# VectorE's weight sums in the Strassen-like FFN, each issued one split later

## The chip, the cores and the metric

One core of a Trainium2 chip runs the whole program in one launch. The metric is the device time in microseconds (us), the median of three runs. Engines are named as in the profile: PE (TensorE), PEld (its weight loads), DVE (VectorE), ACT (ScalarE), POOL (GpSimd), SP (the queue that issues most loads).

## The reference

Two layers act on x (256 tokens x 2048, float32): a token mixer (gated linear attention in the first, sparse attention in the second), then a SwiGLU FFN with 5632 hidden columns.

```python
for i in range(DEPTH):
    h = rmsnorm(x, norm_mix[i])
    x = x + mixer_i(h)
    x = x + swiglu(rmsnorm(x, norm_ffn[i]), ffn_w1[i], ffn_w3[i], ffn_w2[i])
return rmsnorm(x, norm_final)

def swiglu(h, w1, w3, w2):
    return (jax.nn.silu(h @ w1) * (h @ w3)) @ w2
```

The change touches the FFN alone.

## The kernel before

**Splitting.** Every float32 weight tile (128 x 2048, 1 MB, loaded by one DMA) is split in two for PE: `wh` is ACT's rounding copy (line 136), `wl` is DVE's remainder `raw - wh` (line 137). A product of a tile is then three matmuls for each 128 rows of it: hi x wh, hi x wl, lo x wh. `wh` and `wl` have three buffers each, plain weight loads (`raw`) four.

**The FFN.** The 11 column blocks of w1 and w3 (512 columns each) go block by block. Block 0 is multiplied plainly. Then come seven *turns*, numbered 0 to 6 in each layer (14 in all). A turn calls `pair` for one block: it forms h @ w1 and h @ w3 together with seven half products by a Strassen-like scheme, which needs sums of weight quarters. The quarters of a turn are four pairs of tiles: `va` (w1 top), `vb` (w3 top), `vc` (w3 bottom), `vd` (w1 bottom), each with tiles 0 and 1. `va` and `vb` stay in buffers of their own (`v0`, `v1`, `v2`, `g3`; which is which alternates by turn), `vc` and `vd` pass through the `raw` buffers.

`pair` is a generator with eight slots. Its products, in order: A11 (with va), F5 (with va after va += vb), F3 (with vc), A12 (with vd), F6 (with va, reloaded with an accumulating DMA), F7 (with vb after vb += vc), a slot without a product, and N22. Between two slots runs one step of other work: in turns 0, 3 and 6 a step of `plain_steps` (another block multiplied plainly, output `half`), in turns 1, 2, 4 and 5 a step of `pieces` (the FFN's second product, output `down`). Each step loads and splits one tile. These eight work tiles of a turn are called work 0 to work 7 here.

**The sums.** DVE makes four full-tile sums in a turn, at line 406: a0 and a1 (va[0] += vb[0], va[1] += vb[1]), which F5 needs, and b0 and b1 (vb[0] += vc[0], vb[1] += vc[1]), which F7 needs. `product` calls `then(c)` right behind `split_w` of tile c, so each sum is traced behind the split of its own product's tile. F6 and N22 get their sums from POOL's accumulating DMAs (line 409).

**What sets the order.** The Tile framework's scheduler takes instructions in traced order as priority and puts each on its engine's queue, ahead of others that it takes to be not ready; the queue then runs strictly in order. The loads on SP's queue wait for the buffer that they overwrite. The `raw` buffers go round: in each turn the order of these loads is work 0, work 1, vc[0], vc[1], work 2, vd[0], vd[1], work 3 and so on. So vd[1] waits for the last reader of vc[0], and work 3 for the last reader of vc[1]; these readers are the split and the sum (b0, b1).

Of the kernel before, what the change touches and what calls it, by code (L numbers as in the profile page):

```python
# [55 lines left out]
def trunk(  # L56
# [7 lines left out]
    nc = tc.nc  # L64
# [47 lines left out]


    side = deque()

    def tick():

        while side:
            try:
                return next(side[0])  # L120
            except StopIteration:
                side.popleft()
# [9 lines left out]
    def split_w(raw, pool=wp):  # L132

        wh = pool.tile([P, 4, NB], F32R, tag="wh", bufs=3 if pool is wp else 1, name="wh")
        wl = pool.tile([P, 4, NB], F32R, tag="wl", bufs=3 if pool is wp else 1, name="wl")
        nc.scalar.copy(wh, raw)  # L136
        nc.vector.tensor_sub(wl, raw, wh.bitcast(F32))  # L137
        return wh, wl

    def gemm_tail(w, c0, parts, pool, done):  # L140

        acc = [acc_p.tile([P, NB], F32, tag="acc", name=f"acc{t}") for t in range(NT)]
        tiles = []
        for gi, (hi, lo, r0) in enumerate(parts):
            raw = wp.tile([P, 4, NB], F32, tag="raw", bufs=RAW, name="raw")
            nc.sync.dma_start(raw, w[r0:r0 + 512, c0:c0 + NB].rearrange("(k p) n -> p k n", p=P))
            wh, wl = split_w(raw, pool if gi == 0 else wp)
            for k in range(4):
                tiles.append((hi, lo, k, wh[:, k, :], wl[:, k, :]))
        for t in range(NT):  # L150
            ts_ = slice(t * P, (t + 1) * P)
            for i, (hi, lo, k, wh, wl) in enumerate(tiles):
                nc.tensor.matmul(acc[t], hi[:, k, ts_], wh, start=i == 0, stop=False)
                nc.tensor.matmul(acc[t], hi[:, k, ts_], wl, start=False, stop=False)
                nc.tensor.matmul(acc[t], lo[:, k, ts_], wh, start=False, stop=i == len(tiles) - 1)
                if t == 0 and i % 2:
                    tick()
            done(t, acc[t])
# [210 lines left out]
    def pair(nrm, wa, wb, c0, turn, done):  # L369

        def src(w, j, c):
            r = j * 1024 + c * 512
            return w[r:r + 512, c0:c0 + NB].rearrange("(k p) n -> p k n", p=P)

        def load(w, j, homes):
            o = []
            for c, (pool, tag, bufs) in enumerate(homes):
                raw = pool.tile([P, 4, NB], F32, tag=tag, bufs=bufs, name=tag)  # L380
                nc.sync.dma_start(raw, src(w, j, c))
                o.append(raw)
            return o

        def product(acc, raws, form, start, stop, then=None):
            for c in range(2):
                wh, wl = split_w(raws[c])
                if then is not None:
                    then(c)
                hi, lo = nrm.forms[form]  # L390
                for j in range(4):
                    k = 4 * c + j
                    for i, (l_, r_) in enumerate(((hi, wh), (hi, wl), (lo, wh))):
                        nc.tensor.matmul(acc, l_[:, k, :], r_[:, j, :], start=start and k == i == 0,  # L394
                                         stop=stop and k == 7 and i == 2, skip_group_check=not start)
                    if j % 2:
                        tick()

        def bank():
            return acc_p.tile([P, NB], F32, tag="acc", name="acc")  # L400

        def sums(tag):
            return nrm.pool.tile([P, NB], F32, tag=tag, bufs=1, name=tag)

        def plus(dst, other):
            return lambda c: nc.vector.tensor_add(dst[c], dst[c], other[c])  # L406

        def plus_dma(dst, w, j):
            return lambda c: nc.gpsimd.dma_start(dst[c], src(w, j, c), accum_op=ALU.add)

        fz = nrm.pool
        stream = [(wp, "raw", RAW)] * 2
        homes = [((fz, "v0", 1), (fz, "v1", 1)), ((fz, "v2", 1), (res, "g3", 1))]
        va = load(wa, 0, homes[turn])
        vb = load(wb, 0, homes[1 - turn])
        b1 = bank()
        product(b1, va, "A11", True, True, plus(va, vb))
        s1 = sums("s1")
        nc.scalar.copy(s1, b1)
        yield  # L420
        b2 = bank()
        product(b2, va, "F5", True, True, plus_dma(va, wb, 1))
        y = sums("y")
        nc.vector.tensor_sub(y, b2, s1)
        yield
        vc = load(wb, 1, stream)
        product(b2, vc, "F3", False, True, plus(vb, vc))
        yield
        vd = load(wa, 1, stream)
        product(b1, vd, "A12", False, True)  # L430
        done("11", b1)
        yield
        b3 = bank()
        product(b3, va, "F6", True, True, plus_dma(va, wa, 1))
        w = sums("w")
        nc.vector.tensor_sub(w, b3, s1)
        nc.vector.tensor_add(w, w, b2)
        done("12", w)
        yield
        product(b3, vb, "F7", False, True)  # L440
        nc.vector.tensor_add(y, y, b3)
        yield
        yield
        product(b3, va, "N22", False, True)
        nc.vector.tensor_sub(s1, s1, b3)
        done("21", s1)
        done("22", y)
        yield

    def plain(nrm, ws, c0, done):  # L450

        for q, w in zip("12", ws):
            acc = [acc_p.tile([P, NB], F32, tag="acc", name="acc") for _ in range(3)]
            for g in range(4):
                raw = wp.tile([P, 4, NB], F32, tag="raw", bufs=RAW, name="raw")
                nc.sync.dma_start(raw, w[g * NB:(g + 1) * NB, c0:c0 + NB].rearrange("(k p) n -> p k n", p=P))
                wh, wl = split_w(raw)
                for bank, form, start, stop in ((0, "A11", True, True), (1, "F7", True, True)) if g < 2 else \
                        ((0, "A12", False, True), (2, "N22", True, True)):
                    hi, lo = nrm.forms[form]  # L460
                    for j in range(4):
                        k = 4 * (g % 2) + j
                        for i, (l_, r_) in enumerate(((hi, wh), (hi, wl), (lo, wh))):
                            nc.tensor.matmul(acc[bank], l_[:, k, :], r_[:, j, :], start=start and k == i == 0,  # L464
                                             stop=stop and k == 7 and i == 2, skip_group_check=not start)
                        if j % 2:
                            tick()
                if g == 1:
                    s1 = nrm.pool.tile([P, NB], F32, tag="s1", bufs=1, name="s1")
                    nc.scalar.copy(s1, acc[0])  # L470
                    nc.vector.tensor_add(s1, s1, acc[1])
                    yield
            nc.vector.tensor_sub(s1, s1, acc[2])
            done("1" + q, acc[0])
            done("2" + q, s1)
# [690 lines left out]
```

## Time and profile before

| what | us |
|---|---|
| median of three runs | 2260.61 (2259.99 to 2260.88) |
| the profiled execution | 2262.72 |
| its span | 2260.9 |
| PE busy in it | 2226.0 (98%) |
| DVE busy | 1576.4 (70%) |
| ACT busy | 1169.4 (52%) |
| DVE's 56 sums at line 406, each | 2.28 |

The profiled execution's time is 1.8 us above its span, and 2.1 us above the median of the runs. A busy PE in this table means that its matmuls overlap without a gap; the idle time that can be won is what the view of waits shows. The 40-slice picture shows PE at 9 tenths or more in all slices but the last, the granted clock at full, and the DMA engines mostly at 7 to 9 tenths in the FFN's slices.

### The profile page before, as it was taken

Reading aid. Unit: us, or ns where it says so; the run is one execution under the profiler, and the core shown is the slowest. Engines: PE = TensorE matmul, PEld = TensorE weight load, DVE = VectorE, ACT = ScalarE, POOL = GpSimd, SP = SyncE. Lnnn points to the kernel's source line nnn. Section 1 sums busy time; section 2 is a strip of 40 time slices with the busy share of each in tenths; the row PEclk is TensorE's granted clock in tenths of the full one; section 3 lists DMA queues with packets and bytes.
Section 4 is the critical chain, followed back from the end, with each engine's and each line's share of the span. In section 5 each row is a group of like instructions: output and inputs, shape, how many; then the busy total and the mean of one; then the engine's idle time right before and its main releaser. Section 6 shows DMA issues by size and latency. Waiting matters only on the chain.

```text
span 2260.9 us, 25126 instructions
## 1 busy us (share of the span) xinstructions
PE 2226.0 (98%) x10247; PEld 1834.7 (81%) x10247; DVE 1576.4 (70%) x1282; ACT 1169.4 (52%) x1046; POOL 100.1 (4%) x147
## 2 busy tenths in 40 slices
PE   9999999999999999999999999999999999999998
PEld 8888888887787887788888888888888778778787
DVE  6546455778878888876555755556887886887874
ACT  5545455555555555555444544555554555555553
POOL 0000000000000000000100000000000000000000
PEclk9999999999999999999999999999999999999999
DMA  8555465597797797795554555457779779779763
GB/s 289 169 170 188 128 229 184 200 290 223 231 290 219 233 276 228 230 264 179 176 181 150 185 169 168 160 194 242 200 212 313 212 217 310 213 219 304 222 203 111
DMA packets 250547, 484.96 MB, mean 214 GB/s; under 512 B 8072, under 2 KB 20704, under 8 KB 250304
## 3 DMA queue, kind: packets, MB, share of 16 engines
q1 hardware_dynamic: 219856, 423.33, 54.3%
q0 software_dynamic: 29568, 58.72, 15.0%
q8 instruction: 80, 1.31, 0.2%
q10 hardware_dynamic: 1008, 1.31, 0.2%
q14 instruction: 35, 0.29, 0.0%
HBM read 481.20 MB, written 2.12 MB: 214 GB/s over the span
## 4 chain that ended last, share of the span: by engine, by line
PE 81%; DVE 11%; DMA 3%; ACT 2%; issue 2%; SPq 0%; POOL 0%; POOLq 0%; ACTq 0%
PE acc L394 15%; PE acc L202 12%; PE acc L204 12%; PE acc L203 12%; PE half L494 9%; DVE wl L137 4%; PE down L552 4%; PE down L553 4%; PE down L551 4%; DMA raw<-in_ffn_w 3%; PE acc L464 3%; DVE v L406 2%; ACT wh L136 2%; DVE g L406 1%; DVE x L558 1%
## 5 line engine op out<-in xcount | busy, mean ns | idle before, releaser
L136 ACT CAST wh<-raw 128x2048 fp32r<-128x2048 f32 x187 | 358.0, 1915 | 439.4 <-PE down L553 164.3
L137 DVE TENSOR_TENSOR wl<-raw,wh 128x2048 fp32r<-128x2048 f32 x187 | 426.8, 2289 | 204.1 <-ACT wh L136 203.9
L193 DVE TENSOR_TENSOR wl<-raw,wh 128x2048 fp32r<-128x2048 f32 (+3 forms) x161 | 349.9, 2176 | 302.2 <-ACT wh L192 302.1
L192 ACT CAST wh<-raw 128x2048 fp32r<-128x2048 f32 (+3 forms) x161 | 291.9, 1816 | 261.5 <-PE acc L204 211.0
L202 PE MATMUL acc<-wh,hh 128*128 128x512 f32 (+3 forms) x832 | 325.5, 391 | 0.0
L204 PE MATMUL acc<-wh,hl 128*128 128x512 f32 (+3 forms) x832 | 317.3, 381 | 0.0
L203 PE MATMUL acc<-wl,hh 128*128 128x512 f32 (+3 forms) x832 | 316.3, 380 | 0.6 <-DVE wl L193 0.6
L137 DVE TENSOR_TENSOR wl<-v,wh 128x2048 fp32r<-128x2048 f32 x102 | 232.8, 2287 | 24.5 <-ACT wh L136 24.4
L136 ACT CAST wh<-v 128x2048 fp32r<-128x2048 f32 x102 | 195.2, 1913 | 76.6 <-PE acc L394 43.4
L552 PE MATMUL down<-wl,g 128*128 128x512 f32 x512 | 201.3, 393 | 13.7 <-DVE wl L137 13.5
L553 PE MATMUL down<-wh,g 128*128 128x512 f32 x512 | 199.6, 390 | 0.0
L551 PE MATMUL down<-wh,g 128*128 128x512 f32 x512 | 198.3, 391 | 0.0
L203 PEld LDWEIGHTS acc<-wl,hh 128*128 128x128 f32 x832 | 156.7, 188 | 29.5 <-issue 1.7
L204 PEld LDWEIGHTS acc<-wh,hl 128*128 128x128 f32 x832 | 156.3, 188 | 29.5
L202 PEld LDWEIGHTS acc<-wh,hh 128*128 128x128 f32 x832 | 156.5, 188 | 28.6 <-issue 1.9
L394 PE MATMUL acc<-wh,fhF 128*128 128x512 f32 x448 | 174.6, 390 | 0.0
L394 PE MATMUL acc<-wl,fhF 128*128 128x512 f32 x448 | 174.3, 389 | 0.0
L394 PE MATMUL acc<-wh,flF 128*128 128x512 f32 x448 | 174.3, 389 | 0.0
L202 PE MATMUL acc<-wh,g 128*128 128x512 f32 x424 | 167.0, 394 | 0.0
L203 PE MATMUL acc<-wl,g 128*128 128x512 f32 x424 | 165.8, 391 | 0.0
L204 PE MATMUL acc<-wh,g 128*128 128x512 f32 x424 | 165.6, 391 | 0.0
L552 PEld LDWEIGHTS down<-wl,g 128*128 128x128 f32 x512 | 96.1, 188 | 39.2 <-DVE wl L137 20.2
(311 smaller groups left out, 3608.5 us busy)
## 6 DMA issues: line engine op xcount, KB each, us to landing
raw<-in_ffn_w SPq DMA_DIRECT2D x208, 1024.0 KB, 7.0
raw<-in_dsa_w_in SPq DMA_DIRECT2D x48, 1024.0 KB, 5.0
v<-in_ffn_w SPq DMA_DIRECT2D x42, 1024.0 KB, 8.4
raw<-in_gla_w_in SPq DMA_DIRECT2D x40, 1024.0 KB, 5.1
v<-in_ffn_w POOLq DMA_DIRECT2D x40, 1024.0 KB, 9.0
raw<-in_gla_w_out SPq DMA_DIRECT2D x16, 1024.0 KB, 5.0
g<-in_ffn_w POOLq DMA_DIRECT2D x16, 1024.0 KB, 13.0
raw<-in_dsa_w_out SPq DMA_DIRECT2D x16, 1024.0 KB, 4.9
```

Source lines behind the costliest of these rows:

```text
L136: nc.scalar.copy(wh, raw)
L137: nc.vector.tensor_sub(wl, raw, wh.bitcast(F32))
L192: a = nc.scalar.copy(wh[:, sl, :n], raw[:, sl, :n])
L193: v = nc.vector.tensor_sub(wl[:, sl, :n], raw[:, sl, :n], wh[:, sl, :n].bitcast(F32))
L202: nc.tensor.matmul(acc[t][:, :n], hi[:, k, ts_], wh[:, k, :n], start=start, stop=False)
L203: nc.tensor.matmul(acc[t][:, :n], hi[:, k, ts_], wl[:, k, :n], start=False, stop=False)
L204: nc.tensor.matmul(acc[t][:, :n], lo[:, k, ts_], wh[:, k, :n], start=False, stop=last)
L394: nc.tensor.matmul(acc, l_[:, k, :], r_[:, j, :], start=start and k == i == 0, stop=stop and k == 7 and i == 2, skip_group_check=not start)
L494: nc.tensor.matmul(acc[bank], l_[:, k, :], r_[:, j, :], start=start and k == i == 0, stop=stop and k == 7 and i == 2, skip_group_check=not ...
L551: nc.tensor.matmul(acc[t], hi[:, k, ts_], wh[:, k, :], start=start, stop=False)
L552: nc.tensor.matmul(acc[t], hi[:, k, ts_], wl[:, k, :], start=False, stop=False)
L553: nc.tensor.matmul(acc[t], lo[:, k, ts_], wh[:, k, :], start=False, stop=last)
```

## The change

The four DVE sums of a turn are no longer traced behind their own tile's split. `plus` puts them into a queue, and `split_w` takes one from it behind the next split, whatever step that split belongs to. So a0 follows the split of va[1], a1 that of work 0, b0 that of vc[1], and b1 that of work 2, in traced order. No instruction is added or removed.

```diff
     side = deque()
+    sums_due = deque()
...
         wl = pool.tile([P, 4, NB], F32R, tag="wl", bufs=3 if pool is wp else 1, name="wl")
         nc.scalar.copy(wh, raw)
         nc.vector.tensor_sub(wl, raw, wh.bitcast(F32))
+        if sums_due:
+            sums_due.popleft()()
         return wh, wl
...
         def plus(dst, other):
-            return lambda c: nc.vector.tensor_add(dst[c], dst[c], other[c])
+
+            return lambda c: sums_due.append(lambda: nc.vector.tensor_add(dst[c], dst[c], other[c]))
```

In the built programs the order of the loads on SP and of POOL's accumulating DMAs is the same before and after. Turn 0 of each layer keeps its order on every engine. The other twelve turns are of two kinds.

**Turns 2, 3, 5, 6 of each layer (eight turns).** The start of turn 2 on DVE, before; `v2_4323` and `g3_4325` are va, `v0_4327` and `v1_4329` vb, `raw_4384` is work 0:

```order
L445 TENSOR_TENSOR s1_3843<-s1_3843,acc_4086 128x512
L406 TENSOR_TENSOR v2_4323<-v2_4323,v0_4327 128x2048
L584 SCALAR_TENSOR_TENSOR u_4287<-u_4287,rstd_3036,y_3912 128x512
L558 TENSOR_TENSOR x03_87<-x03_87,down0_4222 128x512
L558 TENSOR_TENSOR x13_88<-x13_88,down1_4223 128x512
L137 TENSOR_TENSOR wl_4364<-g3_4325,wh_4363 128x2048
L219 TENSOR_TENSOR g0_4322<-tr_4343,g0_4322 128x512
L406 TENSOR_TENSOR g3_4325<-g3_4325,v1_4329 128x2048
L219 TENSOR_TENSOR g0_4322<-tr_4356,g0_4322 128x512
L137 TENSOR_TENSOR wl_4387<-raw_4384,wh_4386 128x2048
L137 TENSOR_TENSOR wl_4416<-v2_4323,wh_4415 128x2048
```

The same place after (work 0 is now `raw_4383`):

```order
L449 TENSOR_TENSOR s1_3842<-s1_3842,acc_4086 128x512
L138 TENSOR_TENSOR wl_4363<-g3_4325,wh_4362 128x2048
L588 SCALAR_TENSOR_TENSOR u_4287<-u_4287,rstd_3036,y_3912 128x512
L562 TENSOR_TENSOR x03_87<-x03_87,down0_4222 128x512
L562 TENSOR_TENSOR x13_88<-x13_88,down1_4223 128x512
L410 TENSOR_TENSOR v2_4323<-v2_4323,v0_4327 128x2048
L222 TENSOR_TENSOR g0_4322<-tr_4342,g0_4322 128x512
L138 TENSOR_TENSOR wl_4386<-raw_4383,wh_4385 128x2048
L222 TENSOR_TENSOR g0_4322<-tr_4355,g0_4322 128x512
L410 TENSOR_TENSOR g3_4325<-g3_4325,v1_4329 128x2048
L138 TENSOR_TENSOR wl_4416<-v2_4323,wh_4415 128x2048
```

Sum a0 has moved behind the split of va[1], and a1 with the second `g` conversion behind the split of work 0. Further on in the same turn, DVE before, with `raw_4451` work 1, `raw_4483` and `raw_4485` vc, `raw_4523` work 2:

```order
L406 TENSOR_TENSOR v0_4327<-v0_4327,raw_4483 128x2048
L406 TENSOR_TENSOR v1_4329<-v1_4329,raw_4485 128x2048
L137 TENSOR_TENSOR wl_4454<-raw_4451,wh_4453 128x2048
L424 TENSOR_TENSOR y_4449<-acc_4414,s1_4380 128x512
L137 TENSOR_TENSOR wl_4488<-raw_4483,wh_4487 128x2048
L137 TENSOR_TENSOR wl_4505<-raw_4485,wh_4504 128x2048
L558 TENSOR_TENSOR x00_81<-x00_81,down0_4382 128x512
L558 TENSOR_TENSOR x10_82<-x10_82,down1_4383 128x512
L137 TENSOR_TENSOR wl_4526<-raw_4523,wh_4525 128x2048
```

and after:

```order
L410 TENSOR_TENSOR v0_4327<-v0_4327,raw_4483 128x2048
L138 TENSOR_TENSOR wl_4454<-raw_4451,wh_4453 128x2048
L428 TENSOR_TENSOR y_4449<-acc_4414,s1_4379 128x512
L138 TENSOR_TENSOR wl_4488<-raw_4483,wh_4487 128x2048
L138 TENSOR_TENSOR wl_4504<-raw_4485,wh_4503 128x2048
L562 TENSOR_TENSOR x00_81<-x00_81,down0_4381 128x512
L562 TENSOR_TENSOR x10_82<-x10_82,down1_4382 128x512
L410 TENSOR_TENSOR v1_4329<-v1_4329,raw_4485 128x2048
L138 TENSOR_TENSOR wl_4525<-raw_4522,wh_4524 128x2048
```

Sum b0 stays, b1 moves behind three splits and the two x updates. PE and ACT keep their order in these turns.

**Turns 1 and 4 of each layer (four turns).** They follow a turn with `plain_steps`. a0 and a1 move in the same way (the split of work 0 now comes ahead of a1 and of four `g` conversions). DVE's middle of turn 1 before, with `raw_3914` work 1, `raw_3946` and `raw_3948` vc, `raw_3986` work 2:

```order
L406 TENSOR_TENSOR v2_3775<-v2_3775,raw_3946 128x2048
L137 TENSOR_TENSOR wl_3917<-raw_3914,wh_3916 128x2048
L137 TENSOR_TENSOR wl_3951<-raw_3946,wh_3950 128x2048
L424 TENSOR_TENSOR y_3912<-acc_3877,s1_3843 128x512
L137 TENSOR_TENSOR wl_3968<-raw_3948,wh_3967 128x2048
L558 TENSOR_TENSOR x00_81<-x00_81,down0_3845 128x512
L558 TENSOR_TENSOR x10_82<-x10_82,down1_3846 128x512
L406 TENSOR_TENSOR g3_3777<-g3_3777,raw_3948 128x2048
L137 TENSOR_TENSOR wl_3989<-raw_3986,wh_3988 128x2048
```

and after:

```order
L138 TENSOR_TENSOR wl_3917<-raw_3914,wh_3916 128x2048
L410 TENSOR_TENSOR v2_3775<-v2_3775,raw_3946 128x2048
L428 TENSOR_TENSOR y_3912<-acc_3877,s1_3842 128x512
L138 TENSOR_TENSOR wl_3951<-raw_3946,wh_3950 128x2048
L138 TENSOR_TENSOR wl_3967<-raw_3948,wh_3966 128x2048
L562 TENSOR_TENSOR x00_81<-x00_81,down0_3844 128x512
L562 TENSOR_TENSOR x10_82<-x10_82,down1_3845 128x512
L138 TENSOR_TENSOR wl_3988<-raw_3985,wh_3987 128x2048
L410 TENSOR_TENSOR g3_3777<-g3_3777,raw_3948 128x2048
```

Both b0 and b1 stand one split later. In these four turns ACT also takes two `g` conversions ahead of its copy of va[1], and PE takes the eight transposes that feed them a few matmuls later.

## The prediction

> **What bounds the kernel now.** First the page's span and PE's busy row, then who PE waits for.
>
> ```profile
> span 2260.9 us, 25126 instructions
> PE 2226.0 (98%) x10247; PEld 1834.7 (81%) x10247; DVE 1576.4 (70%) x1282; ACT 1169.4 (52%) x1046; POOL 100.1 (4%) x147
> ...
> PE down L552 <- DVE wl L137: 13.5, 12, 1.6
> PE half L494 <- DVE wl L137: 7.3, 6, 1.6
> ```
>
> PE is idle for 34.9 us of the span, and 20.8 us of that in 18 waits, all at the first matmul of a work step that needs `wl` from DVE. Nothing else in the FFN makes PE wait for longer than a pipeline step, so only these 18 waits can be won back by reordering DVE. Next, where they are (timeline of PE):
>
> ```profile
> 531.76 0.50 PE L552 MATMUL down<-wl,g 128*128 128x512 f32 x1 [1.35 <-DVE wl L137]
> 616.77 0.50 PE L552 MATMUL down<-wl,g 128*128 128x512 f32 x1 [1.58 <-DVE wl L137]
> ...
> 1801.35 0.50 PE L552 MATMUL down<-wl,g 128*128 128x512 f32 x1 [0.47 <-DVE wl L137]
> ...
> 2109.59 0.50 PE L494 MATMUL half<-wl,fhA 128*128 128x512 f32 x1 [1.59 <-DVE wl L137]
> ```
>
> Twelve are at work 0, one in each turn but a layer's first: eight of 1.58 to 1.59 us (turns 2, 3, 5, 6; first and last shown are at 616.77 and 2109.59) and four of 1.35 to 1.39 us (turns 1 and 4; 531.76). The other six (1801.35 is one) are at work 3 and hold the rest, 20.8 − 8 x 1.59 − 4 x 1.37 = 2.6 us. Now DVE through the start of turn 2, where I follow the change:
>
> ```profile
> 604.16 0.68 DVE L445 TENSOR_TENSOR s<-s,acc 128x512 f32<-128x512 f32 x1
> 604.76 2.28 DVE L406 TENSOR_TENSOR v<-v,v 128x2048 f32<-128x2048 f32 x1
> 606.96 0.74 DVE L584 SCALAR_TENSOR_TENSOR u<-u,rstd,y 128x512 f32<-128x512 f32 x1
> 607.62 1.27 DVE L558 TENSOR_TENSOR x<-x,down 128x512 f32<-128x512 f32 x2
> 608.82 2.28 DVE L137 TENSOR_TENSOR wl<-g,wh 128x2048 fp32r<-128x2048 f32 x1
> 611.02 0.68 DVE L219 TENSOR_TENSOR g<-tr,g 128x512 fp32r<-128x512 f32 x1
> 611.62 2.28 DVE L406 TENSOR_TENSOR g<-g,v 128x2048 f32<-128x2048 f32 x1
> 613.83 0.69 DVE L219 TENSOR_TENSOR g<-tr,g 128x512 fp32r<-128x512 f32 x1
> 614.43 2.28 DVE L137 TENSOR_TENSOR wl<-raw,wh 128x2048 fp32r<-128x2048 f32 x1
> 616.63 2.28 DVE L137 TENSOR_TENSOR wl<-v,wh 128x2048 fp32r<-128x2048 f32 x1
> 618.84 2.28 DVE L137 TENSOR_TENSOR wl<-g,wh 128x2048 fp32r<-128x2048 f32 x1
> 621.04 4.49 DVE L406 TENSOR_TENSOR v<-v,raw 128x2048 f32<-128x2048 f32 x2
> 625.44 2.28 DVE L137 TENSOR_TENSOR wl<-raw,wh 128x2048 fp32r<-128x2048 f32 x1
> 627.64 0.68 DVE L424 TENSOR_TENSOR y<-acc,s 128x512 f32<-128x512 f32 x1
> 628.25 4.48 DVE L137 TENSOR_TENSOR wl<-raw,wh 128x2048 fp32r<-128x2048 f32 x2
> 632.65 1.27 DVE L558 TENSOR_TENSOR x<-x,down 128x512 f32<-128x512 f32 x2
> 635.04 2.29 DVE L137 TENSOR_TENSOR wl<-raw,wh 128x2048 fp32r<-128x2048 f32 x1 [1.12 <-ACT wh L136]
> ```
>
> DVE runs 30 us here without a gap: four sums fall together with nine splits. A full tile takes 2.28 us and lets the next start after 2.20; the small ones take 0.60 to 0.66. The split of work 0 (614.43) ends at 616.71, and PE starts 0.06 us later: sums a0 and a1 stand ahead of it. PE issues a matmul every 0.227 us and had issued three others after 614.34, so it could have gone on at 615.03: 1.74 us lost. Three more rows of PE, the first matmul with `wl` of work 1, 2 and 3:
>
> ```profile
> 627.78 0.50 PE L552 MATMUL down<-wl,g 128*128 128x512 f32 x1
> ...
> 638.56 0.39 PE L552 MATMUL down<-wl,g 128*128 128x512 f32 x1
> ...
> 649.44 0.39 PE L552 MATMUL down<-wl,g 128*128 128x512 f32 x1
> ```
>
> Work 1's is 0.2 us behind DVE's end at 627.72 and its pace; with the uneven step behind each stall, a turn of this kind loses about 2.1 us in all.
>
> **The change, part by part.** No instruction is added; 48 of the 56 sums move, 2.28 us each, so DVE's busy time stays. What counts is which split DVE finishes when.
>
> *Turns 2, 3, 5, 6, work 0 and 1.* I lay turn 2 out again in the new order with the steps above, from 604.16: s1; split of va[1] 604.76; u 606.96; x 607.62; a0 608.82; first `g` 611.02; split of work 0 611.62 to 613.90; second `g` 613.82; a1 614.42; splits of va 616.62 and 618.82; b0 621.02; split of work 1 623.22 to 625.50. ACT must keep up, since it needs a0 and a1 before it copies the new va:
>
> ```profile
> 611.40 1.92 ACT L136 CAST wh<-v 128x2048 fp32r<-128x2048 f32 x1 [0.80 <-ACT g L218]
> 613.22 0.57 ACT L218 CAST g<-tr 128x512 fp32r<-128x512 f32 x1
> ...
> 644.05 1.91 ACT L136 CAST wh<-raw 128x2048 fp32r<-128x2048 f32 x1 [0.64 <-PE down L553]
> ```
>
> a0 ends at 611.10, before ACT's copy at 611.40; the cast at 613.22 ends at 613.79, before the second `g`; a1 ends at 616.70, and ACT's copy of va[1], 1.9 us, at 618.7, just before its split at 618.82. So work 0 is there 1.1 us before 615.03, and that stall is gone. PE then wants work 1 at 627.6 − 2.0 = 625.6: it is there at 625.50. I count the gain up to here as 2.0 us a turn.
>
> *Work 2.* y goes at 625.5, the splits of vc at 626.2 and 628.4, the x updates at 630.7 (PE's matmuls for them end then, 2 us earlier than at 632.65), b1 at 631.9, the split of work 2 from 634.1 to 636.4. PE wants it at 638.56 − 2.0 = 636.5. The late b1 stands right ahead of it and uses up the cover: 0.1 us is left, and any slip shows here as a stall.
>
> *The loads.* SP's queue, and two windows around a hole between two accumulating loads (the last columns are PE's clock, the DMA engines' busy share and GB/s):
>
> ```profile
> 627.75 3.17 SPq L381 DMA_DIRECT2D raw<-in_ffn_w  x2
> 632.75 15.92 SPq L544 DMA_DIRECT2D raw<-in_ffn_w  x5
> ...
> 628.00:630.00 2.00, 2.00 (x10) 1.62 (x10) 2.00 (x2) 1.26 (x1) 0.43 (x1) 1.00 0.42 86
> 630.00:632.00 2.00, 2.00 (x11) 1.65 (x10) 2.00 (x2) 0.00 (x0) 0.87 (x1) 1.00 1.00 385
> ```
>
> vd[0] and vd[1] are issued when the splits of work 1 and vc[0] free their buffers, work 3 (first of the five) behind the split of vc[1], at 632.75. After the change vd goes 2.1 to 2.2 us earlier, but work 3 has to wait for b1's end at 634.2: 1.4 us later, 3.4 later against PE. Work 3 must land 4.3 us (ACT 1.9, DVE 2.3, handing on 0.1) before PE's 649.44 − 2.0. ACT took it at 644.05, when it had just landed; needed is 643.1. In the DMA engines' order work 3 runs behind vd[1] on the same queue, and the engines are full from 630 on, so its landing follows the work ahead of it. The hole (0.42 of 2 us busy, 1.2 us free) is filled by the earlier vd, which brings the landing to about 642.9: no stall in this turn. Turns with less room lose some: in turn 9 (1801.35) PE already waits 0.47 there, so with 1.2 us from the hole it would lose 2.0 − 1.2 = 0.8 of its lead. Between 0 and 0.8 I take 0.3, since only this one of the eight shows a wait there before. If the landing stayed where it was, this turn would lose 0.9 and turn 9 all 2.0, some 1.3 in the mean; if it followed the issue, 1.4 more, about 2.5.
>
> Sum: 8 x (2.0 − 0.3) = 13.6 us.
>
> *Turns 1 and 4.* Work 0's split, now ahead of a1, comes 2.2 us earlier or more and wins the 1.35 us of 531.76, 1.5 with the uneven step behind it. But here the loads are already late (SP, ACT and PEld in turn 1):
>
> ```profile
> 541.95 2.57 SPq L381 DMA_DIRECT2D raw<-in_ffn_w  x2
> 550.73 13.93 SPq L544 DMA_DIRECT2D raw<-in_ffn_w  x5
> ...
> 554.14 1.92 ACT L136 CAST wh<-raw 128x2048 fp32r<-128x2048 f32 x1 [1.73 <-DMA raw<-in_ffn_w]
> 560.02 1.91 ACT L136 CAST wh<-raw 128x2048 fp32r<-128x2048 f32 x1 [3.97 <-DMA raw<-in_ffn_w]
> ...
> 564.32 0.19 PEld L552 LDWEIGHTS down<-wl,g 128*128 128x128 f32 x1 [0.45 <-DVE wl L137]
> ```
>
> Work 3 is issued at 550.73, behind b1; vd[1] lands just before 554.14, work 3 just before 560.02, and PE waits 0.45. Now b1 goes behind the split of work 2: issue at about 552.6. That is still ahead of vd[1]'s landing, so I take the landing as unmoved; PE then comes 1.5 us earlier and waits 1.5 us longer. Gain 0; bounds +1.5 (it lands early enough) and −1.9 (it lands as much later as it is issued), four times.
>
> Here the Trainium skill bears, page "DMA: Bandwidth & Descriptors", section "Queues, rings and completion order": each DMA engine takes turns packet by packet between the queues that have work. By that rule, too, work 3 would land as its predecessors and POOL's load let it, and the four turns would give 0; the 5.9 us between the two landings, with POOL's load beside, agree.
>
> *The rest.* POOL's accumulating loads wait for the F5 splits of va (616.63 before, 616.62 now): not moved. Turn 0, the mixers and the tail keep their order: 0. Behind work 3 every split waits for PE's buffers, so a lead holds to the turn's end.
>
> From the profiled execution 2262.7 − 13.6 = 2249.1; its 2.1 us over the median are taken off: **2247 us**, −0.6%.
>
> **Rivals.**
> 1. *The loads cap the gain.* The hole isn't filled in time and work 3 lands where it did: 8 x (2.0 − 1.3) = 5.6 us, 2255. For it: the 0.47 at 1801.35 and 0.45 at 564.32. Against it: vd is released 2 us earlier.
> 2. *Everything is won.* Work 3 lands early in all twelve turns: 8 x 2.0 + 4 x 1.5 and the 2.6 of the six waits there, 24.6 us, 2236. The Trainium skill gives a way to it (same page, "Anatomy of one DMA"): 2.0 us plus bytes over 436 GB/s, by estimate 4.4 us for 1 MB. The trace differs: 9.3 us from 550.73 to 560.02. Little speaks for it.
> 3. *Slower.* Work 3's landing follows its issue. Then turns 1 and 4 lose 4 x 1.9 = 7.6, and the eight others end at 8 x (2.0 − 2.5) = −4: 2272. It turns slower where the landing moves by over about 1 us in all twelve turns. Against it: at its new issue its predecessor is still on the way.
> 4. *Nothing.* DVE's chain simply stalls PE later, at work 1 and 2, where I left 0.1 us: 2260 to 2263. Against it: DVE makes one sum less ahead of work 0 and one less ahead of work 1, and has 1.12 us of idle time at 635.04 to absorb.
>
> **How the numbers follow.** My sum 0.62; rival 1 0.16; rival 2 0.08; rival 3 0.06; rival 4 0.08. About 0.2% (4.5 us) is what a measurement of this kernel can tell from no change. Faster: my sum, rival 2 and most of rival 1, 0.84; the same: rival 4 and the rest of rival 1, 0.10; slower 0.06. The sum's own range is 2243 to 2252 (0.2 to 0.6 us a turn either way); with rival 1 and part of 2, leaving out 3, 4 and the ends, 2240 to 2256.
>
> **What would show it.** In the profile after, DVE's L410 and busy times are unchanged; PE's waits for `wl` at work 0 are gone in all twelve turns; what is left sits at work 3, 1 to 2 us in turns 1 and 4 and under 1 in most others, behind ACT copies that wait for a DMA. Stalls at work 1 or 2 would show rival 4; at work 3 over 2 us, rival 3. The prediction fails if DMA landings move by more than 1 us against my account, in either direction.

## The result, and the profile after

The changed kernel takes 2242.96 us in the median of four runs (2241.94 to 2246.99), the kernel before 2260.46 (2259.99 to 2260.88) beside it: a ratio of 0.9926 (95% interval 0.9909 to 0.9943), 17.5 us less. The forecast was 2247. The profiled execution after is the slowest of its four, 2246.99 us against 2262.72: 15.7 us less between the two traces, which are what the turns below are read from.

The page of the kernel after, its span and PE's row:

```profile
span 2245.2 us, 25136 instructions
...
PE 2222.0 (99%) x10247; PEld 1834.7 (82%) x10247; DVE 1573.2 (70%) x1282; ACT 1170.6 (52%) x1046; POOL 100.1 (4%) x147
```

PE's waits after (total us, number, longest):

```profile
PE down L556 <- DVE wl L138: 7.1, 7, 1.6
...
PE half L498 <- DVE wl L138: 1.6, 5, 0.6
```

20.8 us in 18 waits have become 8.7 us in 12. DVE's busy time is the same to about 3 us: it does the same work in another order. Where the twelve are, PE's timeline tells; of turn 2 it also shows the first matmul with `wl` of work 0, 1, 2 and 3:

```profile
563.61 0.50 PE L556 MATMUL down<-wl,g 128*128 128x512 f32 x1 [0.78 <-DVE wl L138]
...
613.87 0.39 PE L556 MATMUL down<-wl,g 128*128 128x512 f32 x1
...
624.98 0.40 PE L556 MATMUL down<-wl,g 128*128 128x512 f32 x1
...
635.88 0.39 PE L556 MATMUL down<-wl,g 128*128 128x512 f32 x1
...
647.64 0.50 PE L556 MATMUL down<-wl,g 128*128 128x512 f32 x1 [0.95 <-DVE wl L138]
...
1790.67 0.50 PE L556 MATMUL down<-wl,g 128*128 128x512 f32 x1 [1.59 <-DVE wl L138]
```

All twelve waits at work 0 are gone, none stands at work 1 or 2, and all that are left are at work 3 (563.61 is turn 1's, 647.64 turn 2's, 1790.67 the longest). Against the rows of before (616.77, 627.78, 638.56, 649.44) turn 2 is ahead by 2.90, 2.80, 2.68 and 1.80 us; 0.69 of that it brings along from the turns ahead, so it wins 2.2 at work 0, still holds 2.0 at work 2, and gives 0.9 back at work 3. Of the 2.2 some 0.45 is order and not time: before, three matmuls without `wl` stood ahead of this one (the two rows below), now one does (at 613.64). So PE's order does change a little in these turns, unlike what the section on the change says.

```profile
614.34 0.61 PE L551 MATMUL down<-wh,g 128*128 128x512 f32 x2
614.80 0.39 PE L394 MATMUL acc<-wh,fhF 128*128 128x512 f32 x1
```

DVE there, after:

```profile
608.13 2.28 DVE L410 TENSOR_TENSOR v<-v,v 128x2048 f32<-128x2048 f32 x1
610.33 0.68 DVE L222 TENSOR_TENSOR g<-tr,g 128x512 fp32r<-128x512 f32 x1
610.93 2.28 DVE L138 TENSOR_TENSOR wl<-raw,wh 128x2048 fp32r<-128x2048 f32 x1
613.13 0.69 DVE L222 TENSOR_TENSOR g<-tr,g 128x512 fp32r<-128x512 f32 x1
613.73 2.28 DVE L410 TENSOR_TENSOR g<-g,v 128x2048 f32<-128x2048 f32 x1
...
622.54 2.28 DVE L138 TENSOR_TENSOR wl<-raw,wh 128x2048 fp32r<-128x2048 f32 x1
```

The split of work 0 (610.93) runs ahead of a1 (613.73). With the 0.69 us added, each row lies within 0.1 us of the layout in the prediction (611.62, 614.42, 623.22).

Taken from the end of one turn to the end of the next (DVE's `s<-s,acc` row, 604.16 before and 603.47 after for turn 2's start), the turns became shorter by:

| turn | layer 1 | layer 2 |
|---|---|---|
| 1 | 0.84 | 0.81 |
| 2 | 0.98 | 1.07 |
| 3 | 1.85 | 1.76 |
| 4 | 1.36 | 1.12 |
| 5 | 2.08 | 0.86 |
| 6 | 1.68 | 1.34 |

The eight turns 2, 3, 5, 6 hold 11.6 us of it, the four turns 1 and 4 hold 4.1; turn 0 and all else come to 0.0 together.

### The profile page after: what moved, and what is told of

It is laid out like the page before. It is cut to its first block, busy times and chain, and to the rows that moved or that the text cites. A ratio compares the mean times of both kernels' runs of the same rounds, so it can differ in the third digit from the quotient of the medians.

```text
span 2245.2 us, 25136 instructions
## 1 busy us (share of the span) xinstructions
PE 2222.0 (99%) x10247; PEld 1834.7 (82%) x10247; DVE 1573.2 (70%) x1282; ACT 1170.6 (52%) x1046; POOL 100.1 (4%) x147
## 3 DMA queue, kind: packets, MB, share of 16 engines
q1 hardware_dynamic: 219856, 423.33, 54.9%
q0 software_dynamic: 29568, 58.72, 15.2%
HBM read 481.20 MB, written 2.12 MB: 215 GB/s over the span
## 4 chain that ended last, share of the span: by engine, by line
PE 83%; DMA 6%; DVE 6%; ACT 3%; issue 1%; SPq 0%; POOL 0%; ACTq 0%; POOLq 0%; DVEq 0%
PE acc L397 17%; PE acc L205 12%; PE acc L207 12%; PE acc L206 12%; PE half L498 10%; DMA raw<-in_ffn_w 6%; PE down L556 4%; PE down L557 4%; PE down L555 4%; DVE wl L138 4%; PE acc L468 3%; ACT wh L137 2%; PE tr L219 1%; DVE v L410 1%; PE trq L901 0%
```

## The experiments

All are edits of the changed kernel unless said otherwise, each timed beside the kernel before (medians of 2260.0 to 2261.7 us), given as a ratio to it. Two theories were on the table. Mine: PE's waits at work 0 went because one sum less stands ahead of that split, and what is left is set by work 3's landing, on DMA engines filled by an accumulating load. The rivals: the later b sums bring part of the gain, or work 3 waits for the plain loads ahead of it in its own queue.

### Which sums matter

With a0 and a1 alone put later:

```diff
+            def add(c):
+                nc.vector.tensor_add(dst[c], dst[c], other[c])
-            return lambda c: sums_due.append(lambda: nc.vector.tensor_add(dst[c], dst[c], other[c]))
+            return (lambda c: sums_due.append(lambda: add(c))) if dst is va else add
```

> Only a0 and a1 are put one split later; b0 and b1 are issued in the code where they were before. In the scheduled order DVE's sequence then equals the changed kernel's everywhere except in turns 1 and 4, where b1 goes ahead of the split of work 2 instead of behind it. Theory (the gain is work 0's split no longer standing behind a1; the b sums bring nothing of their own): 2243 us, within 2 us of the changed kernel; in turns 1 and 4 a wait of about 0.9 us at work 2 takes the place of the same amount at work 3. Rival (the later b sums bring part of the gain): 2248 to 2256 us. Rival by the prediction's account of turns 1 and 4 (b1's place sets work 3's issue, and its landing the turn): with b1 early again, work 3's issue is as before and turns 1 and 4 win 0.5 to 1 us more, 2239 to 2241 us.

Measured: 2245.34 us (2241.11 to 2245.87), ratio 0.9928 (0.9915 to 0.9940). The whole gain is there. The reverse, b0 and b1 alone, was not run, since in the built program the order of every engine is then the one of the kernel before. It is the scheduler that moves b1 behind three splits, as soon as the a sums stand later; the line in the code does not decide it. So in the eight turns DVE's order in this run is the changed kernel's, and the run does not say what b1's place there is worth. An estimate from turn 2 of the changed kernel: the split of work 1 ends at 624.82 and PE uses it from 624.98; with b1's 2.2 us still ahead of it, PE would wait about 2 us there. In the four turns where b1 does differ, PE loses 0.3 us at work 2 and less at work 3 than after the change, and the turns end alike. Work 3 is issued at 550.54 in turn 1, as in the changed kernel (550.58): b1's place does not set it, and the rival that let these turns win more is out.

With a1 alone (`dst is va and c == 1` as the condition):

> Only a1 is put one split later; a0 stands where it was before the change, ahead of the split of va[1]. In the scheduled order work 0's split is then again ahead of a1, and DVE's order from there on is that of the run with both a sums moved. Theory (work 0's split had 1.74 us of lateness and one sum of 2.2 us taken from ahead of it is enough): 2243 us, within 2 us of the changed kernel, no wait at work 0. Rival (both a sums must move, since va[1]'s first split comes 2.2 us later with a0 ahead of it and PE then waits there): 2250 us or more.

Measured: 2245.11 us (2241.39 to 2247.33), ratio 0.9929 (0.9916 to 0.9941). PE's waits in this run:

```profile
PE down L564 <- DVE wl L138: 2.8, 7, 0.7
PE half L506 <- DVE wl L138: 2.7, 3, 1.1
```

None is at work 0. One sum of 2.2 us out of the way is enough for a split that came 1.74 us late; in the code the other three need not move. The theory held, and it is narrower than the change. But in this run's trace, too, DVE has b1 behind the same three splits in the eight turns, so b1 did move.

### Turns 1 and 4 alone

The sums go later only where `turn in (1, 4)`:

> The sums are put one split later in turns 1 and 4 of each layer alone; the other turns keep the order of the kernel before. Theory (from the two traces turn by turn: turns 1, 4 of both layers end 0.84, 1.36, 0.81 and 1.12 us shorter): 4.1 us faster than before, about 2256.4 us, with the four waits at work 0 gone and the eight of 1.58 us left. Rival (the prediction's step: what is won at work 0 is lost again at work 3, net 0): 2260.5 us.

Measured: 2257.61 us (2256.10 to 2260.43), ratio 0.9989 (0.9980 to 0.9998), 0.5 to 4.5 us faster. By its trace the four turns are 0.86, 1.13, 0.70 and 0.35 us shorter than before, 3.0 in all. So the prediction's 0 for them was wrong, by somewhat less than the 4.1 us that the trace of the full change shows.

### What work 3 waits for

Without the second of the two accumulating loads behind F5, so that an addend of F6 and N22 is left out:

```diff
-        product(b2, va, "F5", True, True, plus_dma(va, wb, 1))
+        product(b2, va, "F5", True, True, lambda c: plus_dma(va, wb, 1)(c) if c == 0 else None)
```

> The changed kernel without the second accumulating load behind F5 (F6 and N22 then read va[1] without that addend): 14 MB less through the DMA engines, 8.7 us or more of them in each turn. Theory: the upper bound of what any placing of this load can bring: no wait at work 3, none at F6, 2231 to 2234 us. Rival (work 3 waits for the plain loads ahead of it): 2241 us or more.

Measured: 2234.67 us (2234.27 to 2234.89), ratio 0.9883 (0.9868 to 0.9898), and no wait for `wl` left in the FFN. The queues and issue groups, first of the changed kernel, then of this run (packets, MB and share of the 16 engines; KB each and median us from issue to landing):

```profile
q1 hardware_dynamic: 219856, 423.33, 54.9%
q0 software_dynamic: 29568, 58.72, 15.2%
...
raw<-in_ffn_w SPq DMA_DIRECT2D x208, 1024.0 KB, 7.8
```

```profile
q0 software_dynamic: 22176, 44.04, 11.7%
...
raw<-in_ffn_w SPq DMA_DIRECT2D x208, 1024.0 KB, 5.7
```

Of the changed kernel's 2245.2 us, 15.2% went into 56 accumulating loads, 6.1 us of all 16 engines each; 54.9% into 423 MB of plain loads, 3.1 us for each tile of 1.05 MB. An accumulating tile takes twice the engines' time of a plain one, and with 14 of them gone the FFN's plain loads land in 5.7 us in the median instead of 7.8. The 8.3 us that this run is faster I take as the most that any placing of this load can bring. The runs also agree within 0.6 us, those of the changed kernel within 5, so the spread from run to run seems to go with this load; how it arises, no run shows.

### Placing that load later

A first hold writes a small mark (a copy of 8 elements a partition) on POOL, ahead of the load. It reads `wl` of vd[0], and so waits for DVE's split of it:

```diff
+                    mark = sm.tile([P, 8], F32, tag="mark", bufs=1, name="mark")
+                    m = nc.gpsimd.tensor_copy(mark, last[0][:, 0, 0:8].bitcast(F32))
+                    with behind((m.ins,)):
+                        f(1)
```

> The changed kernel, with one wait more on POOL: the second of the two accumulating loads behind F5 (into va[1]) is held until DVE has split vd[0], some 9 us later. No instruction of the other engines moves. Theory (the accumulating load beside vd and work 3 takes the DMA engines' time and sets work 3's landing): work 3 lands 2 us earlier or more in every turn, the twelve waits there (about 10 us of lost issue time) go, the load lands near 649 us in turn 2, well ahead of F6's split of va[1]; 2232 to 2235 us. Rival A (work 3's landing follows from the plain loads ahead of it in its own queue, and the accumulating load beside matters little): 2241 to 2244 us. Rival B (the held load comes too late for F6 and makes a new wait there of 2 us or more in each turn): 2250 us or slower.

Measured: 2318.58 us (2317.08 to 2318.86), ratio 1.0255 (1.0241 to 1.0269). SP and POOL in turn 2, PE at F6, and four windows there (busy time of PE, PEld, DVE, ACT and POOL, PE's clock, DMA share, GB/s):

```profile
649.41 7.14 SPq L562 DMA_DIRECT2D raw<-in_ffn_w  x4
...
653.88 2.32 POOL L423 COPY mark<-wl 128x8 f32<-128x8 f32 x1 [17.84 <-DVE wl L138]
656.15 1.29 POOL L414 DMA_DIRECT2D g<-in_ffn_w  x1
...
673.13 0.49 PE L398 MATMUL acc<-wh,fhF 128*128 128x512 f32 x1 [1.97 <-ACT wh L137]
675.46 0.50 PE L398 MATMUL acc<-wl,fhF 128*128 128x512 f32 x1 [1.83 <-DVE wl L138]
...
672.00:674.00 2.00, 0.49 (x1) 0.19 (x1) 0.89 (x1) 2.00 (x2) 0.70 (x1) 1.00 0.31 24
674.00:676.00 2.00, 0.55 (x2) 0.50 (x3) 2.00 (x3) 2.00 (x2) 0.00 (x0) 0.97 1.00 169
676.00:678.00 2.00, 2.00 (x6) 1.52 (x6) 2.00 (x2) 0.69 (x1) 0.00 (x0) 0.50 1.12 206
678.00:680.00 2.00, 2.00 (x8) 1.58 (x7) 2.00 (x2) 0.14 (x1) 0.00 (x0) 0.68 0.80 137
```

The load left at 656.15, landed at 671.10, and PE stood still at F6 for 1.97 and 1.83 us, with one matmul between, which cost 4.2 us of issue time. Then it came back at a granted clock of 0.50: six matmuls in 2 us. Before the change, waits of 1.6 us caused no such drop. But a single wait of 1.83 us did in another run (the short hold everywhere, below), where one of 1.82 us did not (PE's rows, and a window behind each, with the same columns as above):

```profile
1704.23 0.76 PE L567 MATMUL down<-wl,g 128*128 128x512 f32 x1 [1.83 <-DVE wl L138]
...
1790.81 0.50 PE L567 MATMUL down<-wl,g 128*128 128x512 f32 x1 [1.82 <-DVE wl L138]
...
1706.00:1708.00 2.00, 2.00 (x7) 1.52 (x6) 2.00 (x2) 0.02 (x1) 1.22 (x1) 0.57 0.97 370
1792.00:1794.00 2.00, 2.00 (x11) 1.62 (x10) 2.00 (x2) 0.61 (x1) 0.64 (x1) 1.00 0.81 294
```

The Trainium skill, page "TensorE: Matmul & The Clock Gate", part 1, has a window of about 3.4 us without work after which PE falls to half its clock. The traces agree on the half, not on the length: neither of the two pauses in turn 2 nor the single one lasted 2.0 us, and why 1.83 us did it and 1.82 us did not is open.

Rival B held, though some 27 of the 76 us that this run is slower than the changed kernel come from the new tile (below). The theory's own part held too: work 3, issued at 649.41, landed at 654.26, in 4.9 us instead of 10.0, and no wait was left there.

The same hold in the kernel before:

> The same hold of the second accumulating load, in the kernel before, without the later sums. Theory: work 0's twelve waits stay, only the six waits at work 3 go (2.6 us, 3.2 us as lost issue time): about 2257 to 2258 us. So the hold is worth about 3 us here and some 9 us on the changed kernel: the later sums moved the bound to the loads. Rival (the loads cost PE the same in both kernels): 8 us or more faster here too, 2252 us or less.

Measured: 2303.66 us (2302.45 to 2305.38), ratio 1.0191 (1.0177 to 1.0205). Both expectations missed. The run tells nothing of what was asked, since late loads at F6 and the tile's shift (below) cover it.

Two shorter holds, to the split of vc[1] and to b1's end:

> The changed kernel; the second accumulating load behind F5 is held until DVE has split vc[1], 1.1 to 1.5 us later than it starts now, instead of 9 us and more as in the run held to vd[0]'s split. Theory (work 3's landing is set by how much of the second accumulating load runs ahead of it): work 3 lands about 1 us earlier, most of the waits there shrink by that, nothing is late at F6 (the load lands near 643 us in turn 2, needed by about 653): 2236 to 2240 us. Rival (any hold is paid back at F6): 2250 us or more. Rival (so short a hold does nothing): 2242 to 2245 us.

> As before it, but held until DVE has made sum b1, which in turns 2, 3, 5 and 6 is when work 3's own load is issued: 5 us later than now there, 7 us later in turns 1 and 4. Theory: work 3 lands about 3 us earlier, all waits there go; the load takes up to 15 us and lands near 648 us in turn 2 (needed by about 653) and near 567 us in turn 1 (needed by about 568): 2232 to 2236 us. Rival (the held load is late at F6 in turns 1 and 4, as in the run held to vd[0]): four waits of 1 to 3 us with a lower clock behind them, 2240 us or more.

Measured: 2271.36 us (2270.43 to 2272.54), ratio 1.0046 (1.0033 to 1.0059), and 2284.02 us (2281.82 to 2286.55), ratio 1.0102 (1.0088 to 1.0116). Both expectations missed, the first one strangely: its waits and PE's busy time are

```profile
PE down L567 <- DVE wl L138: 2.0, 4, 1.1
...
PE 2255.6 (99%) x10247; PEld 1838.5 (81%) x10247; DVE 1577.7 (69%) x1282; ACT 1171.3 (52%) x1046; POOL 110.2 (5%) x161
```

PE waits 6.7 us less than after the change, and yet the kernel is 28 us slower: PE is busy for 33.6 us more with the same 10247 matmuls, and over 6 us of that were lost ahead of the first FFN turn, where no hold is (block 0's last `s<-s,acc` on DVE starts at 446.73, after the change at 440.25). The new tile was left as the suspect. Of the second run it explains most, but not the waits at F6 in turns 1 and 4, of up to 1.8 us, which the rival had named.

### A tile of 32 bytes

The changed kernel with an unused tile, no instruction added:

```diff
+            if turn == 0:
+                sm.tile([P, 8], F32, tag="mark", bufs=1, name="mark")
```

> The changed kernel with the small tile of 32 bytes a partition added and never used; no instruction is added or moved, only the tiles behind it lie 32 bytes further. Theory (the shift alone slows PE's matmuls): 2268 to 2276 us, the matmuls of the mixers and of the products 4 to 7 ns longer in the mean, those of the down projections unchanged, since their operands lie ahead of the new tile. Rival (POOL's marks or the hold did it): 2243 us.

Measured: 2270.22 us (2269.06 to 2270.39), ratio 1.0044 (1.0030 to 1.0058), 27 us over the changed kernel. Groups by line (count, busy us, mean ns), first of the changed kernel, then of this run:

```profile
L205 PE MATMUL acc<-wh,hh 128*128 128x512 f32 (+3 forms) x832 | 325.4, 391 | 0.0
...
L555 PE MATMUL down<-wh,g 128*128 128x512 f32 x512 | 199.3, 392 | 0.0
L397 PE MATMUL acc<-wl,fhF 128*128 128x512 f32 x448 | 174.4, 389 | 0.0
...
L205 PE MATMUL acc<-wh,g 128*128 128x512 f32 x424 | 167.0, 394 | 0.0
```

```profile
L205 PE MATMUL acc<-wh,hh 128*128 128x512 f32 (+3 forms) x832 | 329.1, 396 | 0.0
...
L555 PE MATMUL down<-wh,g 128*128 128x512 f32 x512 | 199.4, 392 | 0.0
L397 PE MATMUL acc<-wl,fhF 128*128 128x512 f32 x448 | 177.2, 395 | 0.0
...
L205 PE MATMUL acc<-wh,g 128*128 128x512 f32 x424 | 167.1, 394 | 0.0
```

Matmuls whose operand `hh` or `fhF` lies behind the new tile take 5 to 6 ns longer; those with `g`, which lies ahead of it, don't. In the built programs `hh` begins at byte 140800 of a partition, 275 x 512; now at 140832, 32 past a multiple of 64. Which alignment it is that counts was not tried. PE's busy time grew by 31.9 us (2222.0 to 2253.9), the kernel by less, since a slower PE no longer waits for any load in the FFN.

### The holds without the new tile

The mark goes into a spare tile that the kernel has:

```diff
-            mark = sm.tile([P, 8], F32, tag="mark", bufs=1, name="mark")
+            mark = pad[:, 0:8]
```

First the short hold everywhere, then the short one in turns 1 and 4 with the long one in all others, then with the short one in turn 0 as well:

> The hold to vc[1]'s split again, but POOL's small mark is written into a spare tile that the kernel already has, instead of into a new one of 32 bytes a partition. In the run with the new tile PE's waits at work 3 shrank and yet its matmuls took 4 to 7 ns longer in some groups everywhere, in the mixers too, where the hold has no part; the new tile had moved all tiles behind it by 32 bytes. Theory (the tile's shift cost that run some 30 us, the hold itself gains): 2236 to 2239 us, matmuls at their old means. Rival (the hold itself slows PE): 2265 to 2272 us as before.

> The mark in the spare tile too; the second accumulating load held to vc[1]'s split in turns 1 and 4, where the longer hold was late at F6, and to b1's end in all others, where it removed every wait at work 3. Theory: 2233 to 2237 us, no wait at F6, at work 3 at most 1 us in each of turns 1 and 4. Rival (the hold itself slows PE): 2260 us or more. Rival (without the slower matmuls PE is earlier and the held load is late at F6 in the eight turns): 2240 us or more, with waits at F6's second tile.

> As the run with two holds, but turn 0 of each layer takes the short hold (to vc[1]'s split) as well, since the long one left waits of 0.69 and 0.81 us at work 3 there and the short one, in the run that used it everywhere, none. Theory: those two waits go, 1.5 to 1.8 us, 2237 to 2238 us; what is left are the four waits of about 0.5 us in turns 1 and 4. Rival (turn 0's waits come from elsewhere, a load just late in both): 2239 to 2241 us.

| hold | us | ratio |
|---|---|---|
| short everywhere | 2241.23 (2240.31 to 2244.25) | 0.9918 (0.9904 to 0.9931) |
| long but in turns 1, 4 | 2239.25 (2238.61 to 2241.29) | 0.9908 (0.9895 to 0.9922) |
| long but in turns 0, 1, 4 | 2243.80 (2240.38 to 2249.15) | 0.9919 (0.9906 to 0.9933) |

PE does not slow down, so the tile was the cause. But all three missed their numbers: the short hold is worth 1.7 us in the medians, with times that overlap the changed kernel's, and the best run wins 3.7 us where 6 to 10 were expected. The third differs from the second in turn 0 alone, and its trace says why it isn't better (POOL, then PE at F6, in turn 2; of the second run POOL in turns 1 and 2):

```profile
632.25 4.32 POOL L428 COPY pad<-v 128x8 f32<-128x8 f32 x1 [13.20 <-DVE v L414]
636.52 1.30 POOL L421 DMA_DIRECT2D g<-in_ffn_w  x1
...
655.01 0.50 PE L400 MATMUL acc<-wl,fhF 128*128 128x512 f32 x1 [1.27 <-DVE wl L139]
```

```profile
547.56 0.19 POOL L428 COPY pad<-wl 128x8 f32<-128x8 f32 x1 [9.46 <-DVE wl L139]
...
633.63 2.12 POOL L428 COPY pad<-v 128x8 f32<-128x8 f32 x1 [13.20 <-DVE v L414]
635.70 1.29 POOL L421 DMA_DIRECT2D g<-in_ffn_w  x1
```

The mark, 8 elements a partition, takes 0.19, 2.12 or 4.32 us, in steps of about one split of DVE's: the long ones all end 0.05 us after the end of one of DVE's full-tile instructions, so the mark waits for DVE. Why it waits for one in one run and for two in another is open. In turns 2 and 5 of both layers it takes 2.12 in the second run; in the third 4.32 in three of these four, and just those three show the F6 wait (1.27, 1.54 and 1.82 us). The Trainium skill, page "GPSIMD Engine Reference", section 1, says that POOL's way into SBUF is shared with VectorE, with contention for instructions of two SBUF inputs, as these splits are. So these holds are not a version to build on: the second run's four times all lie below the changed kernel's four, the third's do not.

## Why the prediction was right, and where it was not

- **Work 0 (eight turns).** Held. The waits went, and the lead over before is 2.0 to 2.2 us in every one of these turns at work 2, where 2.0 was forecast. That moving a1 alone in the code does it was not foreseen.
- **Work 1 and 2 without a stall, 0.1 us of cover at work 2.** Held: no wait in any of the eight turns. Rival 4 is out.
- **Lead lost at work 3.** Mis-sized, and for the wrong reason: 0.3 us in the mean was taken, 0.6 measured (lead of 2.1, 1.45 left), within the bounds of 0 and 0.8. The step that failed is "its landing follows the work ahead of it", vd[1] on the same queue. Before, it did: work 3 landed 2.5 to 3.7 us behind vd[1]. After, vd[1] lands earlier by 5.3 us in the mean of these turns, and work 3 by 0.9 alone, 6.0 to 8.3 us behind vd[1]. It now lands 0.8 to 2.3 us behind the second accumulating load instead, which itself lands 1.1 us later in the mean than before; without that load it lands 4.9 to 5.2 us after its issue, as the run above shows. So the 0.9 lies near the forecast 1.2 by luck. And the spread is wide, from 0.2 later (turn 5 of layer 2) to 2.0 earlier (turn 5 of layer 1), and in turn 2, from which the estimate was made, it did not move at all: 39.8 us from the turn's start, before and after. One turn was a poor sample of transfers that meet differently each time. Nor are the eight turns of one kind: in turns 3 and 6 no x updates stand ahead of b1, and work 3 is issued 28.6 us from the turn's start as before; only in turns 2 and 5 does it go out later, at 29.8. The term came to 11.6 us in the two traces, not 13.6.
- **Turns 1 and 4 at 0.** Wrong, +4.1 us by the traces, and the step that failed is "issue at about 552.6 … I take the landing as unmoved". SP, DVE and ACT after, in turn 1:

```profile
539.70 5.37 SPq L384 DMA_DIRECT2D raw<-in_ffn_w  x2
550.58 6.97 SPq L548 DMA_DIRECT2D raw<-in_ffn_w  x4
...
548.26 2.29 DVE L138 TENSOR_TENSOR wl<-raw,wh 128x2048 fp32r<-128x2048 f32 x1 [0.19 <-ACT wh L137]
550.47 2.28 DVE L410 TENSOR_TENSOR g<-g,raw 128x2048 f32<-128x2048 f32 x1
...
559.32 1.91 ACT L137 CAST wh<-raw 128x2048 fp32r<-128x2048 f32 x1 [5.62 <-DMA raw<-in_ffn_w]
```

  Work 3 is issued at 550.58, not 552.6. With b1 behind the split of work 2, the buffer given to work 3 is no longer vc[1]'s, which waits for b1 (the row at 550.47, to 552.75), but that of work 2, free at the end of its split (550.55). The buffers went out in the order in which they were released, and the forecast kept the old assignment. And the first of the vd loads, which the forecast moved by 2 us in the eight turns, moves here too (541.95 to 539.70), and the second lands 2.4 us earlier for it (554.04 to 551.68), which I left out. The second accumulating load, which shares the DMA engines with vd, lands 1.1 to 2.2 us earlier in these turns, and work 3 lands 1.6 to 2.0 us behind it (1.2 to 1.3 before). So work 3 lands earlier, by 0.85, 1.35, 0.82 and 1.11 us from the start of its turn, though its issue is where it was (550.73 before); the four turns are shorter by 0.84, 1.36, 0.81 and 1.12. Gain and landing are the same number: these turns are bound by that load, as the prediction said, but the load moved. Whether an issue at 552.6 would have undone it, no run shows.
- **The sum.** −13.6 against −15.7 between the two traces: 2.0 too much in one term, 4.1 too little in the other, which hide each other in part: that the total came out near is partly luck. The rest of the 17.5 us between the medians is spread between runs: the profiled execution lies 4.0 us over its median, where 2.1 were taken off. The median lies at the edge of the sum's own range (2243).
- **Rivals.** Rival 1 describes turn 2 and not the mean. Rival 2's end, 2236, would have needed the loads out of the way: 2234.67 without the accumulating load. The fit that rival 2 takes from the Trainium skill, page "DMA: Bandwidth & Descriptors", section "Anatomy of one DMA", is one for loads that GpSimd issues, as that section says; work 3 is SP's. Rival 3 is out: work 3's issue did not move in turns 1, 3, 4 and 6, and in turn 2 the landing stayed where it was though the issue came 1.2 us later from the turn's start.
- **What would show it.** The waits left are 0.78 to 1.00 us in turns 1 and 4, where 1 to 2 was written; in the eight others six are under 1 or gone, as written, and two are 1.01 and 1.59 (the latter in turn 2 of layer 2, the prediction's turn 9).
- **Two readings.** DVE's 30 us without a gap hold seven splits, not nine. The 0.45 at 564.32 is PEld's wait, the weight load's; PE's own there is 0.03. Nothing in the sum rests on either; the second is weaker support for rival 1 than was written.

## What to carry to other kernels

A sum that is not due soon can stand behind a split that is late; look for the one instruction whose length exceeds the lateness (2.2 against 1.74 us), and move that, then see in the scheduled order what else moved with it. When such a wait is gone, the next thing late sets the gain, here a load: work its landing out for several turns, not for one, ask which buffer it will be given in the new order, and ask which other queue's load it shares the DMA engines with. Before a gain from an added wait or mark is judged, see in the groups by line whether matmuls that have nothing to do with it kept their mean.

## What the hardware showed unexpectedly

- A tile of 32 bytes a partition, unused, made the matmuls with operands behind it 5 to 6 ns longer (389 to 395, 391 to 396) and the kernel 27 us slower (2242.96 to 2270.22).
- A POOL copy of 8 elements a partition took 0.19 us, or 2.12 or 4.32 beside DVE's splits and sums, and what was queued behind it started as much later.
- An accumulating load took 6.1 us of all 16 DMA engines for 1.05 MB, a plain one 3.1; beside one, work 3 took 10.0 us to land in turn 2, without it 4.9 to 5.0.
- After two pauses of 1.97 and 1.83 us with one matmul between, PE's granted clock was 0.50 for 2 us and 0.68 for the next two. After a single pause of 1.83 us it was 0.57 for two stretches of 2 us; after another of 1.82 us, and after those of 1.59 us before the change, it stayed at full.
